# One set of tiles for the residual rows and for the attention loop's buffers: a two-layer encoder on one core of Trainium2

## The chip, the cores and the metric

The kernel runs on one core of one Trainium2 chip. The metric is the device time of one execution in microseconds (us), given as the median of several runs. Smaller is better.

## The reference, cut to what matters

The reference is a two-layer encoder trunk in float32 on 1024 tokens of width 1024. The change lies between the first two sub-layers, so these count here:

```python
qkv = h @ w_qkv                                   # h = rmsnorm(x): 16 query heads, 4 key/value heads of 64
q, k = rope(rmsnorm(q)) * 64 ** -0.5, rope(rmsnorm(k))
p = softmax(q @ k.T)                              # per head, 1024 x 1024
x = x + (p @ v) @ w_o                             # the first residual add
x = x + memory_cross_attention(rmsnorm(x), ...)   # into 256 memory rows
x = x + conv_gated_ffn(rmsnorm(x), ...)
```

The second layer does the same with a pooling mixer in place of the attention, and a final RMSNorm ends it.

## The kernel before, in words

Every full-precision product is made from three passes with split operands (`mm3`, lines 759 to 761): a high and a low part of each factor, high made on ACT (line 672 or 680), low on DVE (line 675 or 681).

**The attention** (`attention`, line 775) has a first part that makes K, V and Q, and then a loop over 16 groups G (two heads by 512 queries each). For each group there are 8 score tiles kt of 128 keys: TensorE makes the scores (line 1234), ACT the exponential into a probability tile `pt` of 128 x 1024 (line 1240), TensorE the product with the values, two tiles at a time in four steps d (`plan_values`, line 1272), and DVE and POOL add the same tiles up for the softmax sum (lines 1281 and 1284). There are six `pt` tiles, in a pool `at` that closes with the loop; `V32`, the joined values, is one tile of 128 x 2048 in the same pool, filled by POOL (line 1215). A `pt` tile is free again when its values product and its sums are done; for the last two tiles of a group the last reader is POOL's line 1284, but for the last group it is line 1272 or 1281.

`plan_sum` ends a group: a product with ones (line 1308), a copy (1312), then a chain through SP's queue, "spread" (1317), a reciprocal on DVE (1321), "park" to DRAM (1326), "back" as a broadcast (1331), then a multiplication on POOL (1335) and the split into high and low (672 and 1343) into `OT`, the left factor of the output projection.

The order of the loop is written out by a planner (`Plan`): every operation has an engine, an estimated cost, what it reads and writes, and what it takes from small pools such as the six places of `pt`. The planner plays the loop through by its own estimates and emits each operation at the time it comes to, so each engine's queue, SP's too, is in that order. An operation that takes a place waits in the plan until enough places are free for all takers that are due earlier.

**The output projection** is `Seven.begin` (line 452), called by `cross`. It runs 16 steps (n, t): column half n, row tile t, in the order

```python
steps = ((0, 0), (0, 2), (1, 0), (1, 2), (0, 4), (1, 4), (0, 6), (1, 6),
         (0, 1), (1, 1), (0, 3), (1, 3), (0, 5), (0, 7), (1, 5), (1, 7))
turns = {3: 0, 4: 2, 6: 4, 8: 6, 10: 1, 12: 3, 15: 5}
```

Each step is a product of 24 matmuls of 128x512 (lines 759 to 761), the add of the result to half of the residual tile X[t] on DVE (line 1752), and a save of that half to DRAM by SP (line 319). After the second half of a row tile come its sum of squares on ACT (line 740), the root on POOL (732, 734), and the normalisation in place on DVE (line 323), which overwrites X[t] and so has to wait until both saves have read it. The table `turns` says after which step's product TensorE transposes which normalised tile (line 328): tile 0 after step 3, tile 2 after step 4, tile 4 after step 6. `extras[5]`, the hook `between`, is empty here.

**The loads.** In `run` (line 2333), after the attention, the eight residual tiles X are opened at the addresses of the closed pool `at` and loaded from DRAM, 512 KB each, at line 2344. The weights of the projection's second column half (`load_rows`, line 710, DMAs at line 694, splits at 680 and 681) are asked for after six of the eight loads, and the gain of the next norm is broadcast at line 725. All DMAs are issued by SP, in order.

Of the kernel before, what the change touches and what calls it, by code (L numbers as in the profile page):

```python
# [10 lines left out]
F32 = mybir.dt.float32  # L11
F32R = mybir.dt.float32r
AF = mybir.ActivationFunctionType
OP = mybir.AluOpType
AX = mybir.AxisListType

P = 128
D = 1024
# [615 lines left out]
class Kernel:  # L634
# [140 lines left out]
    def attention(self):  # L775
# [422 lines left out]

        ring, spare = sets[1]
        R.put(spare)  # L1200
        with tc.tile_pool(name="at", bufs=1, reuse_waits="tile") as at, self.psum("psl", 0, 0) as self.ps:
            first = [at.tile([P, 1024], F32, name="pt", bufs=6) for _ in range(6)]
            V32 = at.tile([P, 2048], F32, name="V32").rearrange("p (k h c) -> p k h c", k=NT, h=NKV)
            ones = at.tile([P, HD], F32, name="ones")
            nc.vector.memset(ones, 1.0)
            T, E, O, acc, ON, RS = {}, {}, {}, {}, {}, {}
# [4 lines left out]
            def plan_v32(s):  # L1211
                v4 = R.tiles[V[s]].bitcast(F32).rearrange("p (k h c) -> p k h c", k=4, h=NKV)

                def emit():
                    nc.gpsimd.tensor_tensor(out=V32[:, 4 * s:4 * s + 4], in0=v4[..., :HD], in1=v4[..., HD:], op=OP.add)
                    R.put(V[s])
                plan.add("pool", 1024, emit, (), [("V32", s)], gives=("half", 2))


            def plan_scores(G, kt):  # L1220
                half, m = GROUPS[G]
                b, done = ("T", G, kt), (m % 2, kt) == (1, NT - 1)
                cols = slice(kt % 4 * P, (kt % 4 + 1) * P)

                def emit(first):
                    if first:
                        T[b] = self.ps.tile([P, 1024], F32, name="pT", bufs=2)
                    q, k = R.v(Q[m // 2, half], 4), [R.v(K[i][kt // 4], 4) for i in range(2)]
                    mr = R.hv((ring, G % 4 // 2))[:, G % 2 * 512:(G % 2 + 1) * 512]
                    for i, j in ((0, 0), (0, 1), (1, 0)) if first else ((2, 0),):  # L1230
                        for x in range(2):
                            left = k[i][rows(x), m // 2, cols] if i < 2 else one[rows(x)]
                            right = q[rows(x), m % 2 * 2 + j] if i < 2 else mr[rows(x)]
                            nc.tensor.matmul(T[b][:, x * 512:(x + 1) * 512], left, right, start=(i, j) == (0, 0), stop=i == 2)  # L1234
                    if done and not first:
                        R.put(Q[m // 2, half])

                def exp():
                    E[G, kt] = at.tile([P, 1024], F32, name="pt", bufs=6)
                    nc.scalar.activation(E[G, kt], T.pop(b), AF.Exp)  # L1240
                plan.add("product", 3, partial(emit, True), (), [b], [("B", b)])
                plan.add("product", 1, partial(emit, False), [("qm", G)], [(b, 1)], (), [("qm", G)], gives=("half", 2) if done else None)
                plan.add("grow", 1024, exp, [b, (b, 1)], [("E", G, kt)], [("pt", ("pt", G, kt))], [b, ("pt", G, kt)])


# [17 lines left out]
            def plan_values(G, d):  # L1263
                half, m = GROUPS[G]
                ks = (2 * d, 2 * d + 1)

                def emit():
                    if d == 0:
                        O[G] = self.ps.tile([P, 512], F32, name="pO", bufs=1)
                    for kt in ks:  # L1270
                        for x in range(2):
                            nc.tensor.matmul(O[G][x * HD:(x + 1) * HD], V32[:, kt, m // 2], E[G, kt][:, x * 512:(x + 1) * 512],  # L1272
                                             start=kt == 0, stop=kt == NT - 1)
                es = [("E", G, kt) for kt in ks]
                plan.add("product", 9.2, emit, [*es, ("V32", d // 2)], ["O"],
                         () if d else [("O", ("O", G))], [("pt", G, kt) for kt in ks] + [("O", G)])
                u, mine = ("acc", G, 0), d < 3 or G == last

                def add():
                    acc[G, d] = self.scr()  # L1280
                    nc.vector.tensor_tensor(out=acc[G, d], in0=E[G, ks[0]], in1=E[G, ks[1]], op=OP.add)

                def more(other):
                    nc.gpsimd.tensor_tensor(out=acc[G, 0], in0=acc[G, 0], in1=other(), op=OP.add)
                if mine:
                    plan.add("add", 1024, add, es, [("acc", G, d)], [("scr", ("acc", G, d))], [("pt", G, kt) for kt in ks], late=4.0)
                if d and mine and (G < last or d == 1):
                    plan.add("pool", 900, partial(more, lambda: acc.pop((G, d))), [u, ("acc", G, d)], [u], uses=[u, ("acc", G, d)], late=8.0)
                for kt in ks if not mine else ():
                    plan.add("pool", 900, partial(more, lambda kt=kt: E[G, kt]), [u, ("E", G, kt)], [u], uses=[u, ("pt", G, kt)], late=5.0)  # L1290
                if d == 3:
                    def out():
                        ON[G] = self.scr()
                        nc.scalar.copy(ON[G][:, :512], O.pop(G))
                    plan.add("copy", 512, out, ["O"], [("on", G)], [("scr", ("on", G))], [("O", G)])
# [64 lines left out]
            def plan_rows(g, k):  # L1360
# [13 lines left out]
                plan.add("copy", 1024, partial(part, 0), [raw], [(raw, 0)], [("half", None)] * (0 if g or k else 8), [raw], late=8.0)  # L1374
                plan.add("add", 1024, partial(part, 1), [raw, (raw, 0)], [(raw, 0)], uses=[raw], late=10.0)

            self.ws = []
            with tc.manual_schedule():
                for s in range(2):
                    plan_v32(s)  # L1380
                steps = [(G, d) for G in range(last + 1) for d in range(4)]
                ahead = iter([(G, n) for G in range(1, last + 1) for n in range(NT)])

                def peak():
                    for it in [next(ahead, None)]:
                        if it:
                            plan_peaks(*it)
                for n, (G, d) in enumerate(steps):
                    peak()
                    plan_scores(G, 2 * d)  # L1390
                    if n < 4:
                        peak()
                    plan_scores(G, 2 * d + 1)
                    peak()
                    if n:
                        plan_values(*steps[n - 1])
                    if G and d == 2:
                        plan_sum(G - 1)
                    if G == last - 1:
                        plan_rows(d // 2, d % 2)  # L1400
                plan_values(last, 3)
                plan_sum(last)
                plan.run()
            R.put(*K[0], *K[1], ring)
        return OT


    def memory_part(self, mT, g, t):
        return (self.R.hv(h).rearrange("p (k n) -> p k n", k=4)[:, :, t * P:(t + 1) * P] for h in mT[2 * g:2 * g + 2])
# [5 lines left out]
    def cross(self, i, X, steps=None, mixer=None, over={}):  # L1415
# [213 lines left out]
        def main():  # L1629
            order, parts = U.order(nf), [(c, m) for c in range(8) for m in range(2)]  # L1630
            if steps:
                U.begin(*steps, lambda: None)
                U.H["T4"] = [R.get(), R.get()]
                over.update({"DVE": 6.5, "ACT": 4.9})
            plan = Plan(R, over, {"scr": 2 if steps else 6, "A": 2, "B": 4, "half": len(R.freed)})
# [697 lines left out]
    def run(self):  # L2333
        nc, R, a = self.nc, self.R, self.a
        OT = self.attention()
        self.ps = self.ctx.enter_context(self.psum("ps", 2, 4))
        ws = [self.ws]
        xp = self.ctx.enter_context(self.tc.tile_pool(name="xres", bufs=1, reuse_waits="tile"))
        X = {t: xp.tile([P, D], F32, name=f"X{t}") for t in (1, 3, 0, 2, 4, 6, 5, 7)}
        X = [X[t] for t in range(NT)]  # L2340
        for t in range(NT):
            if t == NT - 2:
                ws.append(self.load_rows(a["attn_w_o"][0], 1))
            nc.sync.dma_start(out=X[t], in_=a["x"][0][t * P:(t + 1) * P, :])

        def lhs(t, k):
            return (R.v(s, 8)[:, k, t % 4 // 2 * P:(t % 4 // 2 + 1) * P] for s in OT[t // 4 * 2 + t % 2])

        def free(t):
            if t % 4 >= 2:  # L2350
                R.put(*OT[t // 4 * 2 + t % 2])

        steps = self.rows_by(lhs, X, free, lambda n, k: self.blk(ws[n], k, slice(0, 512)), lambda n: R.put(*ws[n]))
        lhs, *ops = self.cross(0, X, steps)
        ready = []
        gemm, add, over = self.ffn(0, lhs, X, *ops, lambda plan: ready.extend([self.pool_weights(plan)]))
        lhs, *ops = self.cross(1, X, None, partial(self.pool_mixer, gemm, add, ready[0]), over)
        self.ffn(1, lhs, X, *ops, out=self.out[0])
# [28 lines left out]
```

## Time and profile before

| what | value |
|---|---|
| median of 3 runs | 2458.26 us (2457.17 to 2458.43) |
| the profiled execution, its own time | 2456.54 us |
| its span, first to last instruction | 2454.7 us |
| PE busy / DVE / ACT / POOL | 99% / 78% / 49% / 17% of the span |
| granted TensorE clock, mean | 0.997 of full speed |

How to read what follows: PE is TensorE's matmuls, PEld its weight loads, DVE VectorE, ACT ScalarE, POOL GpSimd, SPq the queue of SyncE that issues the DMAs. A row of the timeline gives the start in us from the beginning of the span, the duration, the engine, the line, what is written and read, and the count; square brackets at its end hold the engine's idle time ahead of it and what ended that. A row of the windows gives a stretch, and for each engine its busy time and count, then the granted clock, the share of the DMA engines' time, and GB/s. The chain of waits gives the pieces of work that each released the next, back from the last instruction.

### The profile page before, as it was taken

The numbers are of one execution on the slowest core, as the hardware profiler recorded it, in microseconds if no ns is written. First come the engines' busy times: TensorE is split into PE (matmuls) and PEld (weight loads), VectorE is DVE, ScalarE is ACT, GpSimd is POOL, SyncE is SP. The second block draws the span as 40 slices with busy tenths as digits, with TensorE's granted clock in tenths as the row PEclk, the third lists the DMA queues.
The fourth block names the chain that finished last, engine by engine and source line by source line (L and its number), as shares of the span: only waits on it lengthen the run. The fifth ranks groups of instructions, "written<-read, shape, count | busy, mean of one in ns | idle before, by whom it ended". The sixth has DMA issues, their size and how long they took to land.

```text
span 2454.7 us, 34706 instructions
## 1 busy us (share of the span) xinstructions
PE 2428.4 (99%) x12814; PEld 1970.4 (80%) x12814; DVE 1914.2 (78%) x2718; ACT 1211.7 (49%) x1942; POOL 428.3 (17%) x457
## 2 busy tenths in 40 slices
PE   9999999999999999999999999999999999999998
PEld 9995555578898888888888888899888888888887
DVE  7888888737965599888889666987479888888875
ACT  6544555524544265545555325556346455545542
POOL 5666777610020100000000003002000000000001
PEclk9999999999999999999999999999999999999999
DMA  4300000233882233432368544497123333338852
GB/s 165 95 19 10 14 15 19 86 121 95 293 282 100 82 91 96 127 108 86 108 226 285 177 128 129 168 312 252 60 67 118 117 107 99 108 102 272 269 189 99
DMA packets 331614, 324.97 MB, mean 132 GB/s; under 512 B 32429, under 2 KB 264221, under 8 KB 331445
## 3 DMA queue, kind: packets, MB, share of 16 engines
q1 hardware_dynamic: 331445, 322.75, 41.1%
q8 instruction: 101, 1.65, 0.3%
q14 instruction: 68, 0.56, 0.1%
HBM read 235.10 MB, written 82.64 MB: 129 GB/s over the span
## 4 chain that ended last, share of the span: by engine, by line
PE 88%; DVE 4%; issue 3%; POOL 2%; DMA 1%; ACT 1%; SPq 0%; POOLq 0%; DVEq 0%; ACTq 0%
PE pB L759 21%; PE pB L761 21%; PE pB L760 21%; PE pT L1234 5%; PE pO L1272 5%; PE pA L761 3%; PE pA L759 3%; PE pA L760 3%; PE pS L791 2%; POOL rs L734 1%; PE pB L328 1%; DVE R L675 1%; PE pS L1308 1%; POOL qn L1032 1%; DVE nm L797 0%
## 5 line engine op out<-in xcount | busy, mean ns | idle before, releaser
L759 PE MATMUL pB<-R,R 128*128 128x512 f32 (+1 forms) x2732 | 1016.3, 372 | 2.5 <-ACT R L672 0.9
L761 PE MATMUL pB<-R,R 128*128 128x512 f32 (+1 forms) x2728 | 1008.3, 370 | 1.4 <-DVE R L675 1.3
L760 PE MATMUL pB<-R,R 128*128 128x512 f32 (+1 forms) x2732 | 1009.4, 369 | 0.2 <-DVE R L675 0.2
L759 PEld LDWEIGHTS pB<-R,R 128*128 128x128 f32 x2732 | 515.7, 189 | 93.1 <-ACT R L672 2.1
L761 PEld LDWEIGHTS pB<-R,R 128*128 128x128 f32 x2728 | 514.6, 189 | 89.7 <-DVE R L675 3.2
L760 PEld LDWEIGHTS pB<-R,R 128*128 128x128 f32 x2732 | 515.8, 189 | 86.5 <-DVE R L675 1.2
L672 ACT ACTIVATE R<-scr 128x512 fp32r<-128x512 f32 (+3 forms) x376 | 272.5, 753 | 227.8 <-DMA scr<-Gs 58.5
L732 POOL TENSOR_SCALAR ms<-ss 128x1 f32<-128x1 f32 (+2 forms) x97 | 31.9, 329 | 1646.2 <-ACT R L740 1281.8
L675 DVE TENSOR_TENSOR R<-X,R 128x512 fp32r<-128x512 f32 x374 | 252.6, 687 | 67.7 <-ACT R L672 67.1
L675 DVE TENSOR_TENSOR R<-scr,R 128x512 fp32r<-128x512 f32 (+2 forms) x332 | 282.6, 879 | 26.8 <-ACT R L672 26.4
L672 ACT ACTIVATE R<-X 128x512 fp32r<-128x512 f32 x374 | 231.8, 630 | 134.5 <-PE pB L760 66.1
L797 DVE TENSOR_REDUCE nm<-pS 128x1 f32<-128x512 f32 x240 | 153.5, 684 | 38.8 <-PE pS L791 38.1
L442 ACT COPY scr<-pB 128x512 f32<-128x512 f32 x156 | 91.1, 584 | 181.8 <-PE pB L761 174.6
L1240 ACT ACTIVATE pt<-pT 128x1024 f32<-128x1024 f32 x128 | 127.1, 1024 | 88.1 <-PE pT L1234 86.0
L1961 DVE TENSOR_TENSOR X<-pB,X 128x512 f32<-128x512 f32 (+1 forms) x145 | 99.3, 686 | 79.6 <-PE pB L761 78.8
L759 PE MATMUL pA<-R,R 128*128 128x512 f32 (+1 forms) x420 | 150.6, 359 | 0.0
L761 PE MATMUL pA<-R,R 128*128 128x512 f32 (+1 forms) x420 | 150.2, 358 | 0.0
L760 PE MATMUL pA<-R,R 128*128 128x512 f32 (+1 forms) x420 | 150.0, 357 | 0.0
L1272 PE MATMUL pO<-pt,V 128*64 128x512 f32 x512 | 123.7, 605 | 0.0
L444 DVE TENSOR_TENSOR scr<-pB,scr 128x512 f32<-128x512 f32 x156 | 107.0, 686 | 11.3 <-PE pB L761 11.0
L1234 PE MATMUL pT<-R,R 64*128 64x512 f32 x768 | 111.9, 393 | 0.2 <-ACT R L1110 0.2
L1806 DVE SCALAR_TENSOR_TENSOR scr<-scr,conv 128x1023 f32<-128x1023 f32 x66 | 84.6, 1282 | 20.8 <-ACT scr L1801 18.9
(188 smaller groups left out, 3065.6 us busy)
## 6 DMA issues: line engine op xcount, KB each, us to landing
X<-in_ffn_w_up SPq DMA_DIRECT2D x82, 512.0 KB
Gs<-X SPq DMA_DIRECT2D x105, 256.0 KB
scr<-in_ffn_w_down SPq DMA_DIRECT2D x45, 512.0 KB
scr<-Gs SPq DMA_DIRECT2D x35, 512.0 KB
scr<-in_xattn_w_kv SPq DMA_DIRECT2D x32, 512.0 KB
scr<-Gs SPq DMA_DIRECT2D x42, 384.0 KB
scr<-in_attn_w_qkv SPq DMA_DIRECT2D x22, 512.0 KB
Wt<-scr SPq DMA_DIRECT2D x44, 256.0 KB
```

The lines of the kernel that those rows point to most:

```text
L442: self.nc.scalar.copy(out, p)
L444: self.nc.vector.tensor_tensor(out=out, in0=p, in1=out, op=OP.add)
L672: self.nc.scalar.activation(hi, src, AF.Copy)
L675: self.nc.vector.tensor_tensor(out=lo, in0=src, in1=hi.bitcast(F32), op=OP.subtract)
L759: mm(out, ah, bh, start=start, stop=False)
L760: mm(out, ah, bl, start=False, stop=False)
L761: mm(out, al, bh, start=False, stop=stop)
L797: nc.vector.tensor_reduce(NM[G][:, 2 * n + x.start:2 * n + x.stop], S, axis=AX.X, op=OP.max, negate=True)
L1234: nc.tensor.matmul(T[b][:, x * 512:(x + 1) * 512], left, right, start=(i, j) == (0, 0), stop=i == 2)
L1240: nc.scalar.activation(E[G, kt], T.pop(b), AF.Exp)
L1272: nc.tensor.matmul(O[G][x * HD:(x + 1) * HD], V32[:, kt, m // 2], E[G, kt][:, x * 512:(x + 1) * 512], start=kt == 0, stop=kt == NT - 1)
L1961: nc.vector.tensor_tensor(out=x, in0=banks[b][:, c], in1=x, op=OP.add)
```

## The change

The residual tiles are opened before the attention loop and outlive it. Two of the eight places hold the values (`V32`, now two tiles, that will be X5 and X7), the other six take the place of the `pt` tiles. Which place an exponential writes is no longer the pool's choice: places are kept in a list, taken from its front, and put at its end when the planner has emitted the last reader. Four new operations of kind "load" in the plan take a place each for good and load a residual tile into it: X0 and X2, planned ahead of the last values step, and X4 and X6, planned behind the last group's sum. The two places that are left over become X1 and X3. X1, X3, X5 and X7 are loaded by the hook `between` of the output projection, in its step 5. In `run` the pool and the eight loads go, and `load_rows` is called straight after the attention.

```diff
+        xp = self.ctx.enter_context(tc.tile_pool(name="xres", bufs=1, reuse_waits="tile"))
+        spots = [xp.tile([P, D], F32, name=f"X{t}") for t in range(NT)]
+        X, spots = dict(zip((5, 7), spots)), spots[2:]
+        self.X = X
         with tc.tile_pool(name="at", bufs=1, reuse_waits="tile") as at, self.psum("psl", 0, 0) as self.ps:
-            first = [at.tile([P, 1024], F32, name="pt", bufs=6) for _ in range(6)]
-            V32 = at.tile([P, 2048], F32, name="V32").rearrange("p (k h c) -> p k h c", k=NT, h=NKV)
+            V32 = [X[t].rearrange("p (k h c) -> p k h c", k=4, h=NKV) for t in (5, 7)]
...
-                    nc.gpsimd.tensor_tensor(out=V32[:, 4 * s:4 * s + 4], in0=v4[..., :HD], in1=v4[..., HD:], op=OP.add)
+                    nc.gpsimd.tensor_tensor(out=V32[s], in0=v4[..., :HD], in1=v4[..., HD:], op=OP.add)
...
-                    E[G, kt] = at.tile([P, 1024], F32, name="pt", bufs=6)
+                    E[G, kt] = spots.pop(0)
                     nc.scalar.activation(E[G, kt], T.pop(b), AF.Exp)
...
+                plan.ended["pt", G, kt] = lambda: spots.append(E.pop((G, kt)))
...
-  nc.tensor.matmul(O[G][x * HD:(x + 1) * HD], V32[:, kt, m // 2], E[G, kt][:, x * 512:(x + 1) * 512],
+  nc.tensor.matmul(O[G][x * HD:(x + 1) * HD], V32[kt // 4][:, kt % 4, m // 2], E[G, kt][:, x * 512:(x + 1) * 512],
...
+            def plan_x(t):
+                def load():
+                    X[t] = spots.pop(0)
+                    self.load_x(t)
+                plan.add("load", 1, load, (), [("X", t)], [("pt", None)], late=0.0)
...
+                for t in (0, 2):
+                    plan_x(t)
                 plan_values(last, 3)
                 plan_sum(last)
+                for t in (4, 6):
+                    plan_x(t)
                 plan.run()
             R.put(*K[0], *K[1], ring)
+            X.update(zip((1, 3), spots))
...
+    def load_x(self, t):
+        self.nc.sync.dma_start(out=self.X[t], in_=self.a["x"][0][t * P:(t + 1) * P, :])
...
-                U.begin(*steps, lambda: None)
+                U.begin(*steps, lambda: [self.load_x(t) for t in (1, 3, 5, 7)])
...
-        xp = self.ctx.enter_context(self.tc.tile_pool(name="xres", bufs=1, reuse_waits="tile"))
-        X = {t: xp.tile([P, D], F32, name=f"X{t}") for t in (1, 3, 0, 2, 4, 6, 5, 7)}
-        X = [X[t] for t in range(NT)]
-        for t in range(NT):
-            if t == NT - 2:
-                ws.append(self.load_rows(a["attn_w_o"][0], 1))
-            nc.sync.dma_start(out=X[t], in_=a["x"][0][t * P:(t + 1) * P, :])
+        ws.append(self.load_rows(a["attn_w_o"][0], 1))
+        X = self.X
```

## The prediction

> **What bounds the kernel now.** I read the page first, then the windows by stage, the chain of waits around the end of the attention loop, and the timelines of PE, DVE, ACT, POOL and SP there.
>
> ```profile
> 191.00:479.00 288.00, 287.51 (x1795) 147.03 (x1796) 242.88 (x314) 153.95 (x187) 200.21 (x103) 1.00 0.10 22
> 479.00:505.00 26.00, 24.77 (x110) 18.61 (x106) 8.79 (x8) 7.87 (x12) 6.61 (x8) 1.00 0.82 294
> 505.00:518.00 13.00, 8.16 (x34) 6.94 (x35) 4.37 (x5) 3.10 (x6) 0.75 (x2) 0.74 0.15 59
> ...
> 590.00:2454.00 1864.00, 1852.16 (x9041) 1562.29 (x9039) 1463.37 (x2000) 919.96 (x1484) 91.21 (x170) 1.00 0.48 154
> ```
>
> TensorE is the bound: in the loop (191 to 479 us) it is busy for 287.51 of 288 us, while DMA moves 22 GB/s, and from 590 us on for 1852 of 1864 us. The only place near the change where TensorE rests is 505 to 518 us: 8.16 of 13 us busy, at a clock of 0.74, right after a stretch in which DMA is busy for 82% of the time. The chain of waits tells why:
>
> ```profile
> 490.65 0.59 SPq L1331
> 491.29 0.57 SPq L2344
> ...
> 492.38 7.53 DMA X<-in_x
> ...
> 500.00 1.30 DVE X L1752 x2
> ...
> 501.32 6.96 DMA Xq<-X
> ...
> 509.84 1.97 PE pB L328 x8
> ```
>
> The loads of the residual stand in SP's queue behind the "back" of the last group's sum (490.65), so the first is issued at 491.29. The adds of steps 1 and 2 (line 1752) wait for them until 500.00, although step 1's product is long done. The save of X0 is then behind the rest of the eight loads and takes 6.96 us; the normalisation of tile 0 (line 323) has to wait for it, and the transposes of tile 0 (line 328) for that. On PE:
>
> ```profile
> 482.37 0.50 PE L759 MATMUL pB<-R,R 128*128 128x512 f32 x1 [0.68 <-ACT scr L1312]
> ...
> 504.06 0.39 PE L761 MATMUL pB<-R,R 128*128 128x512 f32 x1
> 509.84 1.97 PE L328 MATMUL pB<-ident,X 128*128 128x128 f32 x8 [5.39 <-DVE X L323]
> ...
> 517.65 0.40 PE L761 MATMUL pB<-R,R 128*128 128x512 f32 x1
> 517.89 1.03 PE L328 MATMUL pB<-ident,X 128*128 128x128 f32 x8
> ...
> 529.71 1.03 PE L328 MATMUL pB<-ident,X 128*128 128x128 f32 x8
> ```
>
> Steps 0 to 3 of the projection run from 482.37 to 504.06 without a pause, then come 5.39 us of rest, transposes that take 1.97 instead of 1.03 us, and a slow start of step 4.
>
> **The change part by part.** *The stall at 504 us.* Its whole price is measured between the last matmuls of steps 3 and 4. Steps 0 to 3 are 96 matmuls, 95 spacings in 504.06 - 482.37 = 21.69 us, 0.2283 each, so 24 take 5.48 us. From the transposes at 517.89 to those at 529.71 lie one set of transposes and two steps: 11.82 us, so one set costs 11.82 - 10.96 = 0.86 us. Undisturbed, the last matmul of step 4 would come 5.48 + 0.86 = 6.34 us after that of step 3; it comes 517.65 - 504.06 = 13.59 us after it. **The stall with its cold restart costs 13.59 - 6.34 = 7.25 us**, which is what the change can win here.
>
> *Does it go?* With X0 and X2 loaded in the loop, the adds wait for their products alone. Step 2 ends its matmuls 24 spacings before step 3, at 504.06 - 5.48 = 498.58. What follows is read off later, undisturbed steps (the add of step 5 and the normalisation of tile 4, and step 6):
>
> ```profile
> 524.46 0.69 DVE L1752 TENSOR_TENSOR X<-pB,X 128x512 f32<-128x512 f32 x1 [3.04 <-PE pB L761]
> 527.33 1.28 DVE L323 SCALAR_TENSOR_TENSOR X<-X,rs,scr 128x1024 f32<-128x1024 f32 x1 [2.18 <-POOL rs L734]
> 529.48 0.39 PE L761 MATMUL pB<-R,R 128*128 128x512 f32 x1
> 529.91 0.69 DVE L1752 TENSOR_TENSOR X<-pB,X 128x512 f32<-128x512 f32 x1 [1.29 <-PE pB L761]
> ```
>
> An add starts 0.43 us after the last matmul (529.48 to 529.91), the normalisation 2.87 us after the add (524.46 to 527.33), when POOL's root is there and not later for the save, and it takes 1.28. For tile 0 that gives 498.58 + 0.43 + 2.87 + 1.28 = 503.16 us, against 504.06 + 0.23 = 504.29 at which PE wants the transposes. It fits, with 1.1 us to spare. Tile 2 (transposed after step 4) has the same distances and one set of transposes more.
>
> *When the four loads go.* They need places, in SP's order.
>
> ```profile
> 479.24 1.21 SPq L694 DMA_DIRECT2D scr<-in_attn_w_o  x2
> ...
> 482.35 1.31 SPq L1317 DMA_DIRECT2D rs<-scr  x2
> 466.78 1.94 PE L1272 MATMUL pO<-pt,V 128*64 128x512 f32 x8
> 470.59 1.92 ACT L1240 ACTIVATE pt<-pT 128x1024 f32<-128x1024 f32 x2
> 470.70 1.94 PE L1272 MATMUL pO<-pt,V 128*64 128x512 f32 x8
> 475.46 3.65 PE L1272 MATMUL pO<-pt,V 128*64 128x512 f32 x16
> ```
>
> The values step at 470.70 frees two places at 472.6, the first half of the 3.65 us at 475.46 two more at 477.3. X0 and X2 can be issued near 473 to 476 and X4 and X6 near 477.5 to 479, ahead of the last group's spread (482.35). Each issue costs SP 0.57 us (491.29), 2.3 us in all.
>
> *What is queued behind them.*
>
> ```profile
> 475.00:480.00 5.00, 5.00 (x28) 1.74 (x26) 2.78 (x3) 2.24 (x3) 0.00 (x0) 1.00 0.01 2
> 498.00:500.00 2.00, 2.00 (x11) 1.65 (x10) 0.28 (x1) 0.00 (x0) 0.51 (x1) 1.00 1.02 418
> 488.77 2.73 DVE L681 TENSOR_TENSOR R<-scr,R 128x1024 fp32r<-128x1024 f32 x2
> 497.08 1.43 POOL L1343 TENSOR_TENSOR R<-scr,R 128x256 fp32r<-128x256 f32 x2 [0.53 <-ACT R L672]
> ```
>
> DMA is idle from 475 to 480 us, and residual loads run at 418 GB/s, 1.25 us for 512 KB. X0 and X2 cost nobody anything; X4 and X6 can push the weight loads of 479.24 and the last sum's chain back by up to 2.5 us. The weights' low parts are ready at 488.77 + 2.73 = 491.50 and wanted at the start of step 2, 504.06 + 0.23 - 10.96 = 493.33 (their second half later): 1.8 us of cover. The last group's OT is ready at 498.51 and wanted in step 4, at 504.29 + 0.86 = 505.15: 6.6 us. I take 0 us, with 0 and 1 as the ends.
>
> *The loads of X1, X3, X5, X7.* They follow the save of step 4. In the shortened kernel step 4's add ends near 517.65 + 0.43 + 0.69 - 7.25 = 511.5 us; the save and the loads are issued by 514.4, and 2.1 MB at 418 GB/s take 5 us: done near 519. They are wanted from step 8 on, four steps later, near 533. The save of step 5 is queued behind them. Its add ends at 524.46 + 0.69 - 7.25 = 517.9 us, tile 4 must be normalised by 529.71 - 7.25 = 522.46, so the save has to land by 521.2. From the add's end to the normalisation is 2.18 us undisturbed, so it lands by 520.1, or, if it has to wait for the loads until 519, by about 521.2. I take 0 us; the ends are 0 and 2, the latter if the loads ran at 290 GB/s, near the 294 of the whole stretch 479 to 505. The Trainium skill ("DMA: Bandwidth & Descriptors", Specifications) gives a limit of about 358 GB/s from HBM for one core; by it the four loads would take 5.9 us, an estimate that would cost some tenths of this part. The 418 GB/s measured here speak against that limit.
>
> *The loop itself.* The 128 exponentials, and what ended the idle time before the instructions on `pt`:
>
> ```profile
> L1240 ACT ACTIVATE pt<-pT x128: 1002/1025/1030, 186.1 to 475.6; 128x1024 f32<-128x1024 f32 x128
> ...
>   PE pT L1234: 86.0, 61
>   issue: 53.9, 179
>   ACT pt L1240: 7.7, 17
>   PE pS L791: 2.0, 3
> 461.97 5.71 POOL L1284 TENSOR_TENSOR scr<-scr,pt 128x1024 f32<-128x1024 f32 x2
> ```
>
> None waits for a sum on DVE or POOL, so none waits for a place. The list gives the places out in the order of release. In the last groups that is the ring's order: POOL's two tiles of group 14 are released by 467.68, before the first two of group 15 (the values step of 466.78 ends at 468.72), and are used again at 470.59, 2.9 us later. Cost 0; the ends are 0 and 0.5 us for each of 15 groups. The two value tiles now lie where the last weights of the first part were, not where its query tiles were:
>
> ```profile
> 183.44 0.28 PE L761 MATMUL pB<-T,R 128*128 128x256 f32 x1
> 183.56 0.60 PE L1104 MATMUL pB<-ident,qst 128*128 128x128 f32 x4
> 184.24 4.71 POOL L1215 TENSOR_TENSOR V<-R 128x1024 f32<-128x1024 f32 x2 [4.29 <-PE pB L1104]
> ```
>
> Those weights are read last at 183.44, ahead of the query transposes at 183.56 that line 1215 waits for now. So the fill starts no later than now: no cost.
>
> **The sum.** -7.25 for the stall, 0 for the loads in the loop, 0 for those in step 5, 0 for the loop. Behind 590 us everything follows from its predecessors, and PE stays the bound, so the gain is kept. The profiled execution took 2456.54 us (span 2454.7, 1.84 around it); it would take 2449.3. It lies 1.72 below the median of 2458.26, so the median becomes 2458.26 - 7.25 = **2451.0 us**.
>
> **The rivals.** *First, the stall shrinks but stays (partial gain).* The spread of the last group is queued behind X4, X6 and the weight loads, or step 5's save behind its loads. For: the covers of 1.1 and 1.8 us are thin, and the chain from the last reciprocal to OT holds POOL and ACT, which tile 0's root and squares follow in order. Against: DMA is idle while the first two loads go.
>
> ```profile
> 502.88 0.56 POOL L734 TENSOR_TENSOR rs<-ms,mh 128x1 f32<-128x1 f32 x1
> ```
>
> If the four loads pushed that chain by their whole 5 us, POOL would be free for tile 0's root at 498.51 + 5 = 503.5; with 0.56 for the root and some 0.3 around it (an estimate) the normalisation starts at 504.4, not 498.58 + 0.43 + 2.87 = 501.9. That is 2.5 us later, less 1.1 of slack: a stall of 1.4. With 2 more for step 5's save the gain is 7.25 - 3.4 = 3.85, giving 2454.4. What a short stall does to the clock is seen here from two sides: after a rest of 0.68 us (482.37) the matmuls come 0.2283 us apart at once, after one of 5.39 us they do not. If a short rest also brought it down, the restart part, 7.25 - 5.39 = 1.86 us, would come on top: 2456.3. The Trainium skill ("TensorE: Matmul & The Clock Gate", Part 1) says the clock falls after an idle window of about 3.4 us; by that rule such a stall would keep the clock, and 2454.4 would stand.
>
> *Second, no change that can be told.* The loads are not issued in the loop because the plan holds them until the very end, so that X0 lands after 497, as now. For: the last of them are due at the end of the plan. Against: two places are free at 472.6, almost 10 us before the last spread. Gain: the four loads that are gone from the queue ahead of the save, 5 us less landing time, unless the late places cost it; within 0.2% if X0 is late by over 3 us: about 2456.
>
> *Third, slower: exponentials wait for places.* If the list hands out one of POOL's two places while another is already free, an exponential waits for line 1284 (5.71 / 2 = 2.9 us each), then the scores, then PE, which has no slack in the loop. With 15 groups this eats the gain from 0.48 us per group on; at 1 us per group it is 2451.0 + 15 = 2466. For: the list is ordered by the plan's estimates. Against: not one exponential waits for a release now, and the order is the same.
>
> **How the numbers follow.** Full gain, 6.3 to 7.8 us: 0.63. Partial or none: 0.25 (0.17 and 0.08). Slower: 0.12. A measurement of this kernel can tell about 0.2%, 4.9 us, from no change. The full gain lies beyond it, and a quarter of the partial one: faster 0.67, same 0.21, slower 0.12. The forecast's own range is 2450.4 to 2452.0; with the runs' scatter of 0.6 and the partial gain to its far end the range is 2449.8 to 2456.6. Beyond it stays the slower case and the smallest gains.
>
> **What would show it.** Right: X loads on SP between 472 and 480 us, the adds of steps 0 and 2 right after their products, the transposes of tile 0 about 0.2 us after the last matmul of step 3 at 1.00 clock, and from there on the same timeline some 7 us earlier. Wrong: exponentials or scores that wait for POOL or DVE in the loop; an idle PE ahead of the transposes of tile 0 or 4, ended by line 323 behind a save; an idle PE at step 2 behind line 681; or a loop that ends later than 479 us.

## The result, and the profile after

| | before | after |
|---|---|---|
| median | 2457.43 us (2455.33 to 2463.11, 10 runs) | 2451.42 us (2449.1 to 2452.11, 10 runs) |
| ratio after / before | | 0.9971, 95% interval 0.9961 to 0.998 |
| profiled execution (span) | 2456.54 us (2454.7) | 2452.11 us (2450.3) |

Both were run side by side. The changed kernel is faster by 0.2 to 0.39%, that is 4.9 to 9.6 us; forecast were 7.25 us and a time of 2451.0. The cause can be read where it was placed, but not all of its steps went as written.

In the changed kernel some lines have moved: 1240 (exponential) is 1243, 1272 (values) 1276, 1281 and 1284 (sums) 1285 and 1288, 1317 (spread) 1321, 1331 (back) 1335, 1343 (OT) 1347, 1752 (add) 1770. The loads of X are issued by line 1424 instead of 2344, and the tiles that were named `pt` are named X. First the windows of the changed kernel, in the same stretches as before:

```profile
191.00:479.00 288.00, 287.54 (x1797) 147.18 (x1796) 243.51 (x314) 154.52 (x187) 200.90 (x103) 1.00 0.12 27
479.00:505.00 26.00, 25.32 (x117) 19.43 (x114) 9.27 (x10) 7.96 (x12) 6.22 (x8) 1.00 0.51 171
505.00:518.00 13.00, 13.00 (x64) 10.82 (x63) 5.31 (x8) 5.20 (x11) 0.76 (x2) 1.00 0.46 162
```

From 505 to 518 us PE is busy for 13.00 of 13 us (before: 8.16) at a granted clock of 1.00 (before: 0.74). The loop has kept its 287.5 us. The hole is gone; the timeline of PE shows how the stretch now runs:

```profile
482.32 0.50 PE L759 MATMUL pB<-R,R 128*128 128x512 f32 x1 [0.69 <-ACT scr L1316]
...
504.03 0.39 PE L761 MATMUL pB<-R,R 128*128 128x512 f32 x1
504.26 1.03 PE L328 MATMUL pB<-ident,X 128*128 128x128 f32 x8
...
510.63 1.03 PE L328 MATMUL pB<-ident,X 128*128 128x128 f32 x8
...
523.09 1.09 PE L328 MATMUL pB<-ident,X 128*128 128x128 f32 x8 [0.50 <-DVE X L323]
```

The projection starts at the same time as before (482.32, was 482.37). The transposes of tile 0 follow the last matmul of step 3 by 0.23 us and take 1.03 instead of 1.97. Ahead of tile 4's transposes stands a rest that before did not have: 0.50 us. Why the first went is in SP's timeline:

```profile
467.65 1.94 SPq L1424 DMA_DIRECT2D X<-in_x  x2
...
475.52 0.39 SPq L1424 DMA_DIRECT2D X<-in_x  x1
...
477.89 0.34 SPq L1424 DMA_DIRECT2D X<-in_x  x1
...
490.39 0.33 SPq L319 DMA_DIRECT2D Xq<-X  x1
...
494.30 17.57 SPq L319 DMA_DIRECT2D Xq<-X  x4
511.92 0.42 SPq L1424 DMA_DIRECT2D X<-in_x  x1
```

Four loads of X go between 467.65 and 478.2, and the first save (line 319) goes at 490.39, 12 us behind the last of them. The other four loads begin at 511.92. On DVE:

```profile
490.29 2.34 DVE L681 TENSOR_TENSOR R<-scr,R 128x1024 fp32r<-128x1024 f32 x2
...
499.02 0.69 DVE L1770 TENSOR_TENSOR X<-pB,X 128x512 f32<-128x512 f32 x1 [4.75 <-PE pB L761]
501.90 1.28 DVE L323 SCALAR_TENSOR_TENSOR X<-X,rs,scr 128x1024 f32<-128x1024 f32 x1 [2.19 <-POOL rs L734]
...
517.19 0.69 DVE L1770 TENSOR_TENSOR X<-pB,X 128x512 f32<-128x512 f32 x1 [3.03 <-PE pB L761]
521.75 1.28 DVE L323 SCALAR_TENSOR_TENSOR X<-X,rs,scr 128x1024 f32<-128x1024 f32 x1 [3.87 <-DMA Xq<-X]
```

The add of step 2 (499.02) waits for its product and not for a load; the normalisation of tile 0 (501.90) waits for the root and not for a save. The normalisation of tile 4 (521.75) still waits for a save.

To compare executions that begin the projection at slightly different times I use one measure: from the first matmul of step 0 to the transposes of tile 4. Before it is 529.71 - 482.37 = 47.34 us, after 523.09 - 482.32 = 40.77: **6.57 us shorter**. The full stall was 7.25.

### The profile page after: what moved, and what is told of

It reads as the page before. It is cut to its first block, busy times and chain, and to the rows that moved or that the text cites. A ratio compares the mean times of both kernels' runs of the same rounds, so it can differ in the third digit from the quotient of the medians.

```text
span 2450.3 us, 34710 instructions
## 1 busy us (share of the span) xinstructions
PE 2428.7 (99%) x12814; PEld 1970.7 (80%) x12814; DVE 1913.1 (78%) x2718; ACT 1214.0 (50%) x1942; POOL 427.4 (17%) x457
## 4 chain that ended last, share of the span: by engine, by line
PE 88%; DVE 4%; issue 3%; POOL 2%; DMA 1%; ACT 1%; SPq 1%; POOLq 0%; DVEq 0%; ACTq 0%
PE pB L759 21%; PE pB L761 21%; PE pB L760 21%; PE pO L1276 5%; PE pT L1237 5%; PE pA L761 3%; PE pA L759 3%; PE pA L760 3%; PE pS L791 2%; POOL rs L734 1%; PE pB L328 1%; DVE R L675 1%; PE pS L1312 1%; POOL qn L1032 0%; PE pA L2291 0%
## 5 line engine op out<-in xcount | busy, mean ns | idle before, releaser
L1243 ACT ACTIVATE X<-pT 128x1024 f32<-128x1024 f32 x128 | 127.3, 1025 | 89.0 <-PE pT L1237 88.0
L1276 PE MATMUL pO<-X,X 128*64 128x512 f32 x512 | 123.8, 605 | 0.0
```

The lines of the kernel that those rows point to most:

```text
L1276: nc.tensor.matmul(O[G][x * HD:(x + 1) * HD], V32[kt // 4][:, kt % 4, m // 2], E[G, kt][:, x * 512:(x + 1) * 512], start=kt == 0, stop=kt ...
```

## The experiments

"Change" means the changed kernel. None of the kernels leaves out part of the computation; one adds work that nobody reads. The ratios of the first four below (odd rows deferred, places shared, odd rows right after the loop, odd rows in step 6) are to ten runs of the kernel before (median 2457.97 us, 2456.22 to 2459.42), those of the other four to fifteen (2457.78, 2454.3 to 2460.12). The measure from step 0 to tile 4's transposes, from the profiled execution of each:

| kernel | from, to (us) | length | shorter than before | median | ratio to before, 95% |
|---|---|---|---|---|---|
| before | 482.37, 529.71 | 47.34 | | | |
| change | 482.32, 523.09 | 40.77 | 6.57 | 2451.42 | 0.9971 (0.9961 to 0.998) |
| change, again | 480.72, 521.45 | 40.73 | 6.61 | 2449.42 | 0.9967 (0.9954 to 0.9979) |
| odd rows deferred, nothing else | 482.68, 524.53 | 41.85 | 5.49 | 2449.82 | 0.9969 (0.9957 to 0.9981) |
| places shared, no loads planned | 481.52, 521.63 | 40.11 | 7.23 | 2448.23 | 0.996 (0.9948 to 0.9973) |
| change, odd rows right after the loop | 482.44, 522.55 | 40.11 | 7.23 | 2448.32 | 0.9963 (0.9951 to 0.9976) |
| change, odd rows in step 6 | 481.01, 521.13 | 40.12 | 7.22 | 2447.9 | 0.9957 (0.9945 to 0.997) |
| the same again | 482.06, 522.17 | 40.11 | 7.23 | 2450.09 | 0.9963 (0.9949 to 0.9976) |
| before, PE kept busy in the stall | 481.40, 527.86 | 46.46 | 0.88 | 2455.32 | 0.999 (0.9982 to 0.9999) |
| change, places from the end of the list | 521.27, 562.80 | 41.53 | 5.81 | 2491.11 | 1.0137 (1.0123 to 1.0151) |

**Which half of the change makes the gain?** The first kernel is the one of before with only the odd rows' loads taken out of the queue. Nothing is shared and nothing is loaded in the loop.

```diff
...
-        for t in range(NT):
-            if t == NT - 2:
-                ws.append(self.load_rows(a["attn_w_o"][0], 1))
-            nc.sync.dma_start(out=X[t], in_=a["x"][0][t * P:(t + 1) * P, :])
+        self.X = X
+        ws.append(self.load_rows(a["attn_w_o"][0], 1))
+        for t in (0, 2, 4, 6):
+            self.load_x(t)
...
-                U.begin(*steps, lambda: None)
+                U.begin(*steps, lambda: [self.load_x(t) for t in (1, 3, 5, 7)])
```

> The kernel before, with one part of the change: after the loop only X0, X2, X4 and X6 are loaded, X1, X3, X5 and X7 in step 5. Buffers are not shared and nothing is loaded in the loop. Theory A (the stall is the queue of eight loads ahead of X0's save): X0 still lands near 497.5 us, but the save is behind four loads fewer, 5 us, so the rest of PE ahead of tile 0's transposes falls from 5.4 to about 0.6 us, the cold restart goes with it, and the kernel is about 6 us faster than before, as good as the whole change within a microsecond. Theory B (X0's late landing itself makes the stall, so the loads in the loop are what counts): a rest of 4 us or more stays and the gain is under 3 us.

SP, DVE and PE of this kernel (the load is line 1409, the add 1755):

```profile
492.60 2.00 SPq L1409 DMA_DIRECT2D X<-in_x  x4
497.99 0.69 DVE L1755 TENSOR_TENSOR X<-pB,X 128x512 f32<-128x512 f32 x1 [5.19 <-DMA X<-in_x]
504.13 1.28 DVE L323 SCALAR_TENSOR_TENSOR X<-X,rs,scr 128x1024 f32<-128x1024 f32 x1 [3.18 <-DMA Xq<-X]
505.47 1.09 PE L328 MATMUL pB<-ident,X 128*128 128x128 f32 x8 [0.69 <-DVE X L323]
524.53 1.09 PE L328 MATMUL pB<-ident,X 128*128 128x128 f32 x8 [0.67 <-DVE X L323]
```

The loads go as late as before (492.60), and the add waits for one until 497.99. Yet the rest ahead of tile 0 is 0.69 instead of 5.39 us, and the transposes take 1.09 instead of 1.97. So a late X0 alone didn't make the stall; the four loads that stood between it and its save did. This half of the change wins 5.49 of the 7.25 us by itself, and by the time it can't be told from the whole. Of what it lacks, 0.85 us arise up to tile 0 (505.47 - 482.68 = 22.79, against 504.26 - 482.32 = 21.94 in the change). The rest arises at tile 4, where the odd rows' loads stand ahead of step 5's save as they do in the change.

**The other half alone.** The change without the planned loads and without the deferral: all eight loads stand in `run` after the attention again, in their old order.

```diff
-                for t in (0, 2):
-                    plan_x(t)
                 plan_values(last, 3)
                 plan_sum(last)
-                for t in (4, 6):
-                    plan_x(t)
                 plan.run()
             R.put(*K[0], *K[1], ring)
-            X.update(zip((1, 3), spots))
+            X.update(zip((1, 3, 0, 2, 4, 6), spots))
...
-                U.begin(*steps, lambda: [self.load_x(t) for t in (1, 3, 5, 7)])
+                U.begin(*steps, lambda: None)
...
-        ws.append(self.load_rows(a["attn_w_o"][0], 1))
         X = self.X
+        for t in range(NT):
+            if t == NT - 2:
+                ws.append(self.load_rows(a["attn_w_o"][0], 1))
+            self.load_x(t)
```

> The change without its new load times: residual tiles serve as probability and value buffers, places given out by the list, but all eight residual tiles are loaded after the loop in the order of before. Theory A (the sharing is neutral): the loop ends at 479 us as before, the rest ahead of tile 0's transposes is 5.4 us as before, the time is that of before within 1 us. Theory C (the list makes exponentials wait): the loop ends later than 479 us by 0.5 us or more per group, over 7 us in all, and the kernel is slower than before. Theory D (the list frees places sooner and helps): the loop ends earlier than 478.5 us.

Every theory missed: it takes the whole gain. SP of this kernel (the load is line 1420), and PE at tiles 0 and 4:

```profile
470.96 1.24 SPq L1420 DMA_DIRECT2D X<-in_x  x2
...
474.67 2.24 SPq L1420 DMA_DIRECT2D X<-in_x  x3
...
478.39 0.33 SPq L1420 DMA_DIRECT2D X<-in_x  x1
...
503.46 1.03 PE L328 MATMUL pB<-ident,X 128*128 128x128 f32 x8
...
521.63 1.03 PE L328 MATMUL pB<-ident,X 128*128 128x128 f32 x8
```

Six of the eight loads are issued from 470.96 to 478.7 without any step in the plan. In the source they stand behind the whole loop, yet in SP's queue they stand among the loop's own transfers: a spread of the loop follows the first two at 473.30. So the queue is not in the order of the source here. SP's waits name the readers of the places: from 465 to 500 us the loads wait 5.6 us for DVE's sum (line 1285) and 2.2 us for the values products (line 1276). In before all eight are issued from 491.29 on, right behind the last "back" (490.09 to 491.24), and SP's waits there show none for line 2344: what held them was their place in the queue.

The two kernels differ in where these tiles lie and when they are opened: before, in the space of a pool that the loop closes at its end; here, in tiles that exist already. That this is what moved the loads forward in the queue is the likely reading; no run tests it apart from the rest of the edit. Both rests are gone although six loads were issued before the first save, because they were issued 14 us or more ahead of it (the save comes at 493.30). The last two loads, at 490.39 and 492.14, stand right ahead of the save and cost no rest.

**Where the odd rows' loads should stand.** Two kernels are the change with the hook moved: in the first the four loads come in `run` right after `load_rows` and step 5's hook is empty, in the second the hook runs in step 6.

```diff
-                U.begin(*steps, lambda: [self.load_x(t) for t in (1, 3, 5, 7)])
+                U.begin(*steps, lambda: None)
...
+        for t in (1, 3, 5, 7):
+            self.load_x(t)
```

> The change with X1, X3, X5 and X7 loaded straight after the weights of the second half, not in step 5. Theory A (every save or broadcast that is queued behind a batch of loads is late by the batch): step 5's collision goes (0.5 us of PE rest and what follows it, 0.75 us together), but the last group's broadcast is now behind 2.1 MB, up to 5 us, so its output is ready near 503 instead of 499 us, POOL reaches tile 0's root late, and PE rests 0 to 1.5 us ahead of tile 0's transposes. Total: 6 to 8 us faster than before, within 1 us of the change. Theory E (the queue has room everywhere before 505 us): no rest at all, 8.0 us faster than before.

Its SP, POOL and PE:

```profile
467.73 5.34 SPq L1424 DMA_DIRECT2D X<-in_x  x3
...
488.98 0.81 SPq L1424 DMA_DIRECT2D X<-in_x  x2
489.89 1.15 SPq L1335 DMA_DIRECT2D scr<-inv  x2
...
497.51 1.44 POOL L1347 TENSOR_TENSOR R<-scr,R 128x256 fp32r<-128x256 f32 x2 [0.53 <-ACT R L672]
522.55 1.03 PE L328 MATMUL pB<-ident,X 128*128 128x128 f32 x8
```

Two loads stand at 488.98, right ahead of the last group's "back" (489.89), and OT is still ready at 497.51 + 1.44 = 498.95 us. The change itself has it at 499.30, before had it at 498.51. The push that the expectation feared does not come, and no rest is left at tile 4. But it was tested with two loads and not with four: of the eight, five are issued by 478.4 us (three of them in the first row above), and the last goes at 491.09, behind the "back".

```diff
-    def begin(self, gemm, add, free, between):
+    def begin(self, gemm, add, free, between, at=5):
...
-        extras = {5: between,
+        extras = {at: between,
...
-                U.begin(*steps, lambda: [self.load_x(t) for t in (1, 3, 5, 7)])
+                U.begin(*steps, lambda: [self.load_x(t) for t in (1, 3, 5, 7)], 6)
```

> The change with its hook in step 6 instead of 5, so that X1, X3, X5 and X7 are loaded behind the save that tile 4's normalisation waits for. Theory A (the 0.5 us rest ahead of tile 4's transposes is that save queued behind the four loads): the rest goes, the timeline stays 7.25 us ahead of before from step 5 on, 0.75 us ahead of the change, about 8.0 less whatever the clock does later: near 2450.5 against 2457.4. Rival F (tile 4's wait has another cause, such as ACT or POOL): the rest stays at 0.5 us. Risk: the odd tiles land too late for step 8; they have 10 us for 5 us of transfer.

Its SP and PE:

```profile
516.97 1.87 SPq L1424 DMA_DIRECT2D X<-in_x  x4
521.13 1.03 PE L328 MATMUL pB<-ident,X 128*128 128x128 f32 x8
```

With the loads behind step 5's save, tile 4's transposes start without a rest. So the 0.50 us there come from the loads that stand ahead of that save, and removing them gives 40.77 - 40.12 = 0.65 us on the measure. Both kernels come within 0.03 us of the 40.09 (47.34 - 7.25) that a vanished stall leaves. That is the whole of it: the 8.0 us of the two expectations counted the collision in step 5 on top of the stall, although before has no rest there.

**Rest or restart?** In before, the price of 7.25 us had a rest of 5.39 and 1.86 of slow restart. This kernel is before with 44 transposes into a tile that nobody reads, between step 3's product and tile 0's transposes:

```diff
+            if u == 0 and warm:
+                idle = self.kn.psA()
+                for _ in range(warm):
+                    self.nc.tensor.transpose(idle[:, :P], self.kn.ident, self.kn.ident)
             if u is not None:
                 self.turn(u)
...
-                U.begin(*steps, lambda: None)
+                U.begin(*steps, lambda: None, 44)
```

> The kernel before, with 44 more transposes of the identity on TensorE between step 3 and the transposes of tile 0 (a result that nothing reads): about 44 x 0.11 = 4.8 us of work inside the 5.4 us rest. Theory A (the stall is 5.39 us of rest and 1.86 us of cold restart, and the restart comes from the rest): the rest shrinks to about 0.6 us, the clock stays at 1.00 from 505 to 515 us, step 4 ends 1.86 us earlier than before although TensorE has more to do, so the kernel is 1 to 2 us faster than before. Rival G (the slow start is something else, or the clock falls for work of that kind too): step 4 ends as before or later, 0 or slower.

PE:

```profile
503.33 4.96 PE L470 MATMUL pA<-ident 128*128 128x128 f32 x44
...
509.63 1.09 PE L328 MATMUL pB<-ident,X 128*128 128x128 f32 x8 [1.33 <-DVE X L323]
...
516.05 1.03 PE L328 MATMUL pB<-ident,X 128*128 128x128 f32 x8
```

The window in which the rest lies:

```profile
505.00:510.00 5.00, 3.67 (x34) 3.44 (x33) 1.71 (x2) 0.00 (x0) 0.00 (x0) 1.00 0.13 52
```

With a rest of 1.33 us the clock stays at 1.00, and from tile 0's transposes to tile 2's it takes 516.05 - 509.63 = 6.42 us, where before needs 517.89 - 509.84 = 8.05 and the change 510.63 - 504.26 = 6.37. So **the restart costs 1.63 to 1.68 us and it comes from the rest**, not from the loads or from contention: before's eight loads are all still there. In before the windows of 1 us show a clock of 0.50 from 507 to 513 us; with 0.82 from 513 to 514 that makes some 3.5 us from the restart at 509.84 on, and half the speed loses 1.8 us of them, an estimate of the same size. In this execution tile 0's transposes also came 0.76 us later after step 0 (509.63 - 481.40 = 28.23, before 27.47), which leaves 0.88 on the measure. They came later because the transfers did: counted from the start of step 0, its add got its load 0.35 us later than in before (496.96 - 481.40 = 15.56, against 497.58 - 482.37 = 15.21), and the normalisation behind the save came 0.76 later (26.89, against 26.13); why the transfers were slower is open. The total, 0.999 of before, agrees with a gain of that small size.

**Which place an exponential takes.** The change with one edit, so that a place is taken from the end of the list, the one given back last:

```diff
-                    E[G, kt] = spots.pop(0)
+                    E[G, kt] = spots.pop()
```

> The change with the list of places read from its other end: an exponential takes the place that was released last, not the one released first. Theory A (order of release gives every place the longest time to be free): now an exponential is given a place whose last reader is still at work on the chip, waits for it for up to 2 us, and TensorE waits with it; the loop ends later than 479 us by 0.5 to 2 us per group, 8 to 30 us in all. Rival H (six places are so many that the order does not matter): the loop ends at 479 us and the time is that of the change.

What ended the waits of instructions on other engines, from 191 to 515 us in this kernel (total us, times, longest):

```profile
ACT X L1243 <- PE pO L1276: 141.5, 55, 3.9
...
ACT X L1243 <- POOL scr L1288: 3.7, 2, 3.0
```

Its first matmul of the projection, on PE:

```profile
521.27 0.50 PE L759 MATMUL pB<-R,R 128*128 128x512 f32 x1 [0.68 <-ACT scr L1316]
```

The waits in the change, 191 to 481 us:

```profile
ACT X L1243 <- PE pT L1237: 85.2, 62, 3.3
...
ACT X L1243 <- PE pO L1276: 0.9, 1, 0.9
```

In the change the exponentials wait for scores, and only one, for 0.9 us, waits for a place. Taken from the end of the list, 55 of them wait 141.5 us for the values product that reads their place: a place is put back when its last reader is emitted, not when that reader is done, so the one put back last is the one still being read. The projection starts 521.27 - 482.32 = 38.95 us later, 2.6 us for each of 15 groups, and the total shows it (2491.11 against 2449.42 for the change in the same runs, 41.69). The price is real and larger than the rival of the prediction had it; it was POOL's line 1288 that the prediction named, and only two waits are for that.

**The two best, again.** Between the medians of the change (2451.42) and of the version with step 6 (2447.9) lay 3.5 us, five times what the measure shows. Both ran once more.

> The change itself once more, on the same chip as its variant with the odd tiles loaded in step 6. From the first matmul of the projection to the transposes of tile 4 it should take 40.8 us, as it did, against 47.3 before. In total 6 to 7.5 us less than before; if what came on top in the variants (2.5 us) was the chip or the clock of those runs, the change shows it here as well and is at 8 to 9.

> The change with the odd tiles loaded in step 6, once more, beside the change itself. Theory A (the two differ by the collision in step 5 alone): 40.1 us from the first matmul of the projection to the transposes of tile 4, against 40.8, and 0.65 us less than the change in total, within the scatter of both. Rival I (the step of the loads also decides what the clock does in the second layer): 3 us or more less than the change, as the medians of the two earlier sessions had it.

PE at tile 4 in the change:

```profile
521.45 1.09 PE L328 MATMUL pB<-ident,X 128*128 128x128 f32 x8 [0.48 <-DVE X L323]
```

and in the version with step 6:

```profile
522.17 1.03 PE L328 MATMUL pB<-ident,X 128*128 128x128 f32 x8
```

The rest is there again in the one and not in the other, and again the lengths differ by 0.62 us. The medians now lie the other way round (2449.42 and 2450.09). So moving the loads to step 6 is worth 0.6 us in the trace, and no more could be told in the total; the 3.5 us did not come back.

## Why the prediction was right, point by point

**The price of the stall (7.25 us): right.** The four executions without any rest come out 7.22 to 7.23 us shorter. Its split, 5.39 of rest and 1.86 of restart, was a little off: the transposes came 509.84 - 504.29 = 5.55 us later than wanted, which leaves 1.70 for the restart, and 1.63 to 1.68 were measured.

**Does it go: right, to the tenth.** Forecast were the add of step 2 at 499.01, the normalisation of tile 0 from 501.88 to 503.16 and PE ready at 504.29; the trace has 499.02, 501.90 to 503.18, and 504.26.

**When the four loads go: wrong in place, right in effect.** The step said that X0 and X2 take the places freed by the values step of 470.70 and go at 473 to 476. They went at 467.65. POOL shows why:

```profile
461.92 5.70 POOL L1288 TENSOR_TENSOR scr<-scr,X 128x1024 f32<-128x1024 f32 x2
```

This sum of group 14 ends at 467.62, and 0.03 us later SP issues. SP's waits confirm it: the first load waits 2.3 us for line 1288, and the second, at 468.77, waits 0.7 us for DVE's line 1285, which ends at 468.71. So the loads took places that were released before the values step of 470.70; the first is one that POOL read last, and the prediction had counted those for the exponentials of 470.59. The exponentials moved on to others, and one of them waits 0.9 us for a place (at 476.54, for line 1276). X4 and X6 went at 475.52 and 477.89, near the forecast.

**What is queued behind them: 0 us, right.** The weights' low parts are ready at 490.29 + 2.34 = 492.63, 1.1 us later than before and still 0.7 ahead of the 493.33 at which they are wanted. The last group's OT:

```profile
497.87 1.43 POOL L1347 TENSOR_TENSOR R<-scr,R 128x256 fp32r<-128x256 f32 x2 [0.53 <-ACT R L672]
```

It is ready at 499.30, 0.8 us later, where the prediction gave it 6.6 us of cover.

**The loads of X1, X3, X5, X7: 0 us was wrong, 0.65 measured; this is the term that was mis-sized.** The prediction needed the save of step 5 to land by 521.2 and counted on the loads being done at 519 at 418 GB/s. The save, in the chain of waits of the changed kernel:

```profile
517.91 3.72 DMA Xq<-X
```

The windows there (the last two columns are the DMA engines' share and GB/s):

```profile
512.00:514.00 2.00, 2.00 (x10) 1.66 (x9) 1.13 (x2) 1.34 (x3) 0.00 (x0) 1.00 0.81 258
...
516.00:518.00 2.00, 2.00 (x11) 1.65 (x10) 0.69 (x1) 0.02 (x1) 0.00 (x0) 1.00 1.01 395
```

It landed at 521.63. The rate of 418 GB/s was taken from two microseconds of a batch already running; in these windows the batch that starts has 258 in its first and 395 at its best. The profile of before already had such a start: with its eight loads under way the DMA engines moved 237 GB/s from 492 to 494 us, 315 from 494 to 496 and only then 406. 521.63 is 0.43 us past the limit, and PE rests 0.50. The result lies inside the term's ends of 0 and 2. The Trainium skill ("DMA: Bandwidth & Descriptors", Specifications) has about 358 GB/s from HBM for one core. The prediction's estimate by it points the right way; but the 395 GB/s here lie above that figure, so it is not what held the loads.

**The loop: 0 us, right,** and the experiment with the list's other end shows that the step was not a formality: with another order it is 39 us.

**The reason given was too narrow.** The text traced the stall to the loads' late issue and to the save behind them, and put its chance on the loads in the loop. The first two experiments show that either remedy is nearly enough by itself: fewer loads ahead of the save (5.49 us), or the shared places, with which the loads go early unplanned (7.23). The four planned loads were not needed for the gain in either.

**The clock after a short rest: the price in the first rival stands, its dearer form (2456.3) falls.** The rests measured here of 0.50, 0.69 and 1.33 us left transposes of 1.09 us and a clock of 1.00, the one of 5.39 us transposes of 1.97 and 0.74. The Trainium skill ("TensorE: Matmul & The Clock Gate", Part 1) puts the idle window at about 3.4 us; these rests lie on both sides of it, and the trace agrees here. It does not agree everywhere: in the second layer a rest of 1.82 us, with more idle time close before it, was enough for a clock of 0.50 (last section), so the length of one rest does not decide it, and 3.4 us is no safe bound in this kernel.

**From the measure to the total.** The two profiled executions differ by 2456.54 - 2452.11 = 4.43 us, less than the 6.57 of the measure. Most of the difference is found in the last section, in a stretch that no edit touches. The ratio of the runs, 0.9971, gives 7.1 us of 2457.43, the medians differ by 6.0; 6.57 and 7.25 both lie in the interval of 4.9 to 9.6, so the runs can't tell the full gain from that less 0.65. That the median of 2451.42 comes within 0.4 us of the forecast is therefore partly luck: the gain in the trace is 0.7 us smaller than the one forecast, and the same kernel measured again gave 2449.42.

## What to carry to other kernels

A small store that others wait for can pay for the large loads that were issued ahead of it and have not landed: 6.96 us behind the loads of before and 3.72 us behind four, while tile 0's save in the changed kernel held nothing up (2.19 us after the add the normalisation starts, and waits for the root); put such loads behind the store, or so early that they have landed. Look in the trace for where a load stands in its queue; in these runs the source did not tell it. With tiles opened behind the loop the loads stood behind the loop's last transfer; with tiles opened ahead of it they were issued when the readers of their places were done, some 20 us sooner. Where places are handed out by a list, take the one that was freed first: the one returned last may still be read.

## What the runs showed of the hardware that was not expected

In a stretch of the second layer that no edit touches (the mixer around 1520 us), the granted clock falls in some executions and stays in others, with the same kernel. The two profiles of the version with step 6, first the earlier one:

```profile
1515.00:1535.00 20.00, 18.71 (x146) 17.60 (x145) 18.22 (x26) 14.60 (x29) 3.44 (x8) 1.00 0.26 107
```

and the later one:

```profile
1515.00:1535.00 20.00, 19.45 (x153) 19.09 (x152) 15.95 (x22) 12.53 (x25) 5.43 (x12) 0.91 0.26 106
```

In the change it stays down longer, after a rest of 0.56 us and a run of narrow matmuls that the records show as busy:

```profile
1518.75 1.06 PE L328 MATMUL pB<-ident,X 128*128 128x128 f32 x8 [0.56 <-DVE X L323]
1519.74 2.29 PE L2291 MATMUL pA<-scr 24*128 24x16 f32 x16
```

The window behind them:

```profile
1522.20:1524.20 2.00, 2.00 (x10) 2.00 (x11) 0.55 (x1) 0.67 (x2) 0.00 (x0) 0.50 0.00 0
```

The clock goes to 0.50 while PE is recorded as busy. It falls at or just behind these narrow matmuls in five of the ten executions, and stays at 1.00 in the other five. Over 1515 to 1535 us the mean is 0.83 in the change and 0.91 in before, so (1 - 0.83) x 20 = 3.4 us of clock are lost there against 1.8. That is 1.6 of the 2.1 us by which the profiled pair differs less than the measure says. That narrow matmuls count as idle for the clock would fit, but no run here tests it, and it stays open.

It would not explain every fall. In two executions the clock also falls some 35 us earlier, where no narrow matmul stands. Here is PE in the kernel with the places shared, which from 1484 to 1486 us is busy for 1.40 of 2 us and from 1486 to 1488 for 0.41, and the window behind that:

```profile
1487.59 0.58 PE L761 MATMUL pB<-R,R 128*128 128x256 f32 x1 [1.82 <-DVE R L675]
```

```profile
1488.00:1490.00 2.00, 2.00 (x11) 2.00 (x11) 0.39 (x1) 0.00 (x0) 1.36 (x2) 0.50 0.35 133
```

In the later profile of the version with step 6 the same rest is 1.41 us and the clock falls too; in the change it is 0.53 us and the clock stays at 1.00.
